# Score products over all 128 rows, a stacked gate product, and one engine for both block inversions in a one-core diffusion trunk step

## The chip, the cores and the metric

The kernel runs on one core of a Trainium2 chip, in one launch. The metric is the time of one execution on the device in microseconds (us), the median of several runs; lower is better.

## The reference, cut to what matters

One inference step of a two-layer trunk over 1152 tokens of width 1024: 128 context tokens and a 64 by 16 grid of 1024 latent tokens. Layer 0 mixes with neighbourhood attention (mixer A, 8 heads of 64) beside a bidirectional gated linear attention (mixer B); layer 1 with windowed grouped-query attention with a sink (mixer C) beside a bidirectional gated DeltaNet (mixer D). Each layer ends in a gated convolutional FFN. What the change touches is this:

```python
# mixers A and C, per block of 128 queries and per head
s = einsum(q, k) * scale (+ bias or mask)      # local keys and 128 cached keys
p = softmax(s);  o = einsum(p, v)

# mixer B: gates of both directions from a rank-16 projection
z = einsum('btzr,zrc->btzc', glr, w_g2) + b_g
g = log_sigmoid(z) / 16

# mixer D: per chunk of 64 tokens, a unit lower triangular solve
m_mat = tril(k_beta @ k.T * gam, -1) + eye(64)
sol = triangular_solve(m_mat, rhs)             # forward and time-flipped
```

Everything is computed to fp32 accuracy.

## The kernel before, in words

**Accuracy.** The large products keep fp32 accuracy by splitting: a value is rounded to fp32r (`hi`), the remainder goes into a second tile (`lo`), and a product is `hi*hi + hi*lo + lo*hi` in three TensorE passes of one array pass each (`gemm8`, lines 156 to 158). Plain fp32 operands make a matmul of two passes, which the trace shows as two records.

**Order of the program.** `even_a` (mixer A), `even_b` (mixer B), half of the output projection, FFN 0, `odd_1` (projections of C and D, preparation of D, block inversions), `odd_2` (mixer C, with the second half of the inversions between its units), `odd_3` (the recurrence of D), output projection, FFN 1. Instructions are written by Python generators; `weave` (line 322) interleaves a main generator with a filling one by the costs that they yield, and `mix` (line 1864) takes turns by fixed numbers. Where `manual_schedule` names an engine, that engine's instructions keep the written order; elsewhere the framework orders them by written priority and its own estimate. Inside a queue (TensorE = PE, VectorE = DVE, ScalarE = ACT, GpSimd = POOL, SyncE = SP, which issues most DMAs) everything runs in order.

**Attention (lines 524 to 643).** A head pair shares 128 partitions, head i on rows 64i to 64i+63. For each head, `stack_q` puts the rounded q on its own 64 rows of `qs[i]` and the remainder on the other 64; `stack_k` puts the rounded k on both halves of `ks[i]`, and the remainder of k on the head's 64 rows of one tile `kl` that the two heads share. `scores` then makes each piece of a score with two products: line 541 over 128 rows (`qs` against `ks`), and line 542 over the head's 64 rows only (`q[r:r+64]` against `kl[r:r+64]`). A unit is one block of 128 queries for two heads: score pieces for head 0, then head 1; DVE adds bias and takes the maximum (596), ACT exponentiates (606), DVE scales (621), PE transposes (630), ACT copies the transposes into a `pt` tile (632, four buffers), PE multiplies with v (641). Per head pair there are nine units: the context block with one piece of 128 keys, block 0 with pieces of 256 and 128, blocks 1 to 6 with 384 and 128, block 7 with one piece of 384. Four head pairs make 36 units in A and 36 in C. With depth 2, a unit's transposes come two units after its scores. In A, projections of the next pair fill between the units, and at the start of each pair the bias tiles are rebuilt from two tables: `rpb` by 8 DMAs (837) into a buffer of its own, the mask by one DMA per head (839), added on DVE (842).

**Gates of B (lines 887 to 970).** `narrow` makes the 32 rows of `glr`, ACT copies them (896) into a tile of 33 rows whose last row is 1 (892); `zgen` multiplies it in plain fp32 with `wz` (33 rows, 945), three pieces for each of two directions and four head pairs: 24 products. The weights of the projections go through the shared tiles `wraw`, `whi` and `wlo`, two buffers each.

**Block inversion of D (`inv`, lines 1362 to 1395).** For each head pair p the 32 by 32 diagonal blocks of 36 chunk matrices are inverted by elimination, 72 blocks on 72 partitions: 31 steps of one multiplication (1390) and one subtraction (1392), for the forward direction (d = 0) on DVE and for the backward one (d = 1) on POOL. `prep` writes the matrices out with POOL DMAs (1360, `am_dram`), `inv` reads the blocks back with SP DMAs (1375, `sysM`), and writes the inverses with POOL DMAs (1395, `n_dram`). The inversion of pair p-1 fills beside the preparation of pair p (`side`, 1413). The last one, `inv(3)`, runs in `odd_1`'s tail beside the last projections and the rotary products (`rope`, 1441 to 1445), with DVE and POOL in written order. The tile `X` of the next `prep` (1290) has the buffer of `am`, so it waits for the `am_dram` DMA. In `odd_2`, `merge` transposes the inverses (1512) and completes them with products (1518) between C's units.

Of the kernel before, what the change touches and what calls it, by code (L numbers as in the profile page):

```python
# [8 lines left out]
F32 = mybir.dt.float32  # L9
# [43 lines left out]
class Net:  # L53
    def __init__(self, ctx, tc, I, O, dbg=None):
# [38 lines left out]
        self.half = {}  # L93
        self.dvec = {n: self.const(f"dvec_{n}", [128, 18, 8]) for n in ("eG", "eE", "dl", "be")}

# [435 lines left out]
    def stack_k(self, ps, src, i, ks, kl, dst):  # L531
        nc = self.nc
        r, o = 64 * i, 64 * (1 - i)
        hi = dst(ks[r:r + 64])
        nc.scalar.copy(hi, src(ps[r:r + 64]))
        nc.scalar.copy(dst(ks[o:o + 64]), src(ps[r:r + 64]))
        nc.vector.tensor_tensor(out=dst(kl[r:r + 64]), in0=src(ps[r:r + 64]), in1=hi.bitcast(F32), op=ALU.subtract)

    def scores(self, s, off, q, ks, kl, r, c0, n, first, last):
        mm = self.nc.tensor.matmul  # L540
        mm(s[:, off:off + n], q, ks[:, c0:c0 + n], start=first, stop=False, skip_group_check=True)  # L541
        mm(s[:, off:off + n], q[r:r + 64], kl[r:r + 64, c0:c0 + n], start=False, stop=last, skip_group_check=True)  # L542

    def attn(self, mp, units, fill, depth=1):
# [5 lines left out]
        while q1 or q2 or not end:  # L550
# [14 lines left out]
            if u is not None:  # L565
                s = []
                for i in range(2):
                    t = self.pmt("s")
                    segs = u["segs"]
                    off = 0  # L570
                    for x, (c0, n) in enumerate(segs):
                        self.scores(t, off, u["q"][i], u["ks"][i], u["kl"], 64 * i, c0, n, x == 0, x == len(segs) - 1)
                        off += n
                    s.append(t)
                u["s"], u["nk"] = s, off
# [192 lines left out]
    def even_a(self, mp):  # L768
# [8 lines left out]
        def proj_a(p):  # L777
            qs = [mp.tile([128, T], F32R, name="qs", tag=f"qs{i}", bufs=2) for i in range(2)]
            ks = [mp.tile([128, 1280], F32R, name="ks", tag=f"ks{i}", bufs=2) for i in range(2)]
            kl = mp.tile([128, 1280], F32R, name="kl", tag="kl", bufs=2)  # L780
            kf = mp.tile([128, 128], F32, name="kf", tag="kf", bufs=1)
            ck = mp.tile([128, 128], F32, name="ck", tag="ck", bufs=1)
            nc.sync.dma_start(ck, I["akT"][p])
# [14 lines left out]
            def ev_k(b, ps):  # L798
                for o, n, t0 in IPIECES[b]:
                    if t0 < TP:  # L800
                        nc.scalar.copy(kf, ps[:, o:o + n])
                        nc.sync.dma_start(self.O["nak"][p], kf)
# [26 lines left out]
        def units():  # L829
            for p in range(4):  # L830
# [3 lines left out]
                bias = [mp.tile([128, 1280], F32, name="bias", tag=f"bias{i}", bufs=1) for i in range(2)]  # L834
                rb = mp.tile([128, 2, 384], F32, name="rpb", tag="rpb", bufs=1)
                for cl in range(8):
                    nc.sync.dma_start(rb[16 * cl:16 * cl + 16], I["rpbx"][2 * p:2 * p + 2, :, (7 - cl) * 16:(7 - cl) * 16 + 384].rearrange("h r k -> r h k"))
                for i in range(2):
                    nc.sync.dma_start(bias[i], I["maskA"])
                    for (b0, n0), (r0, n) in zip(VAR, ((0, 384), (128, 256), (0, 256))):  # L840
                        d = bias[i][:, b0:b0 + n]
                        nc.vector.scalar_tensor_tensor(out=d, in0=rb[:, i, r0:r0 + n], scalar=8.0, in1=d, op0=ALU.mult, op1=ALU.add)
                oT = mp.tile([128, T], F32, name="oT", tag="oT", bufs=1)
# [43 lines left out]
    def even_b(self, mp):  # L887
        nc, I = self.nc, self.I
        mm = nc.tensor.matmul
        self.wq = nc.scalar  # L890
        glr = mp.tile([33, T], F32, name="glr", tag="glr", bufs=1)
        nc.vector.memset(glr[32:33, :], 1.0)

        def glr_ev(b, ps):
            for o, nn, t0 in IPIECES[b]:
                nc.scalar.copy(glr[0:32, t0:t0 + nn], ps[:32, o:o + nn])

        wz = mp.tile([33, 2, 512], F32, name="wz", tag="wz", bufs=1)
        nc.sync.dma_start(wz, I["wz"])
        rst = mp.tile([128, T], F32, name="rst", tag="rst", bufs=1)  # L900
# [292 lines left out]
    def odd_1(self, mp, zp):  # L1193
# [168 lines left out]
        def inv(p):  # L1362
# [15 lines left out]
            for jj in range(31):  # L1378
                for d in range(2):
                    M, N, tmp = sy[d]  # L1380
                    eng = nc.vector if d == 0 else nc.gpsimd
                    if d == 0:
# [87 lines left out]
    def odd_2(self, mp, zp):  # L1470
# [17 lines left out]
        ks = [mp.tile([128, 1280], F32R, name="ks", tag=f"cks{i}", bufs=1) for i in range(2)]  # L1488
        kl = mp.tile([128, 1280], F32R, name="kl", tag="ckl", bufs=1)
        ck = mp.tile([128, 128], F32, name="ck", tag="cck", bufs=1)  # L1490
# [770 lines left out]
def build(tc, I, O):  # L2261
    with ExitStack() as ctx:
# [3 lines left out]
        def popen(name):  # L2266
            st = ExitStack()
            return st, st.enter_context(tc.tile_pool(name=name, bufs=1))
# [8 lines left out]
        for l in range(2):  # L2277
            if l:
                with tc.tile_pool(name="mz", bufs=2) as zp:
                    with tc.tile_pool(name="md", bufs=2) as mp:  # L2280
                        n.odd_1(mp, zp)
                    with tc.tile_pool(name="mc", bufs=2) as mp:
                        n.odd_2(mp, zp)
# [48 lines left out]
            ns.close()  # L2332
            xs.close()
        banks.close()

# [24 lines left out]
```

## Time and profile before

| what | us |
|---|---|
| median of 3 runs (3481.23 to 3495.96) | 3494.06 |
| the profiled execution | 3488.37 |
| its span in the profile | 3485.9 |
| PE busy / PE weight loads busy | 3321.6 / 3074.4 |
| DVE busy / ACT busy / POOL busy | 2035.4 / 1427.7 / 810.3 |
| mean granted TensorE clock of the profiled execution | 0.968 |

A granted clock of 1.00 is 2.4 GHz and 0.50 is 1.2 GHz; a value between is a mix over the stretch. An engine's share of the whole span says little here, because the stages have different limits; each is read by itself. In rows of the timeline the difference between the starts of two products is what a product costs in the queue; the length printed beside it overlaps the next one.

### The profile page before, as it was taken

Reading aid. Unit: us, or ns where it says so; the run is one execution under the profiler, and the core shown is the slowest. Engines: PE = TensorE matmul, PEld = TensorE weight load, DVE = VectorE, ACT = ScalarE, POOL = GpSimd, SP = SyncE. Lnnn points to the kernel's source line nnn. Section 1 sums busy time; section 2 is a strip of 40 time slices with the busy share of each in tenths; the row PEclk is TensorE's granted clock in tenths of the full one; section 3 lists DMA queues with packets and bytes.
Section 4 is the critical chain, followed back from the end, with each engine's and each line's share of the span. In section 5 each row is a group of like instructions: output and inputs, shape, how many; then the busy total and the mean of one; then the engine's idle time right before and its main releaser. Section 6 shows DMA issues by size and latency. Waiting matters only on the chain.

```text
span 3485.9 us, 58431 instructions
## 1 busy us (share of the span) xinstructions
PE 3321.6 (95%) x23095; PEld 3074.4 (88%) x23095; DVE 2035.4 (58%) x4040; ACT 1427.7 (41%) x3259; POOL 810.3 (23%) x1064
## 2 busy tenths in 40 slices
PE   6999999999999999999899977999989999999997
PEld 4988787889999999999798876777889999999997
DVE  5244577557555555555757776665676554444556
ACT  3345445545644444442554444551353222222223
POOL 1000001102644554450306585002310000000002
PEclk8999998999999999999999988999999999999999
DMA  5311233143322222221224444206410111111111
GB/s 178 100 55 43 72 116 105 58 159 111 93 82 83 85 77 80 83 89 47 85 73 116 113 121 126 52 15 219 153 46 29 44 43 37 42 44 43 43 43 67
DMA packets 186235, 285.18 MB, mean 82 GB/s; under 512 B 84043, under 2 KB 128203, under 8 KB 185836
## 3 DMA queue, kind: packets, MB, share of 16 engines
q1 hardware_dynamic: 152716, 228.03, 20.6%
q10 hardware_dynamic: 29264, 38.69, 3.6%
q0 software_dynamic: 3984, 14.75, 1.6%
q8 instruction: 183, 3.00, 0.4%
q14 instruction: 88, 0.72, 0.1%
HBM read 233.04 MB, written 48.37 MB: 81 GB/s over the span
## 4 chain that ended last, share of the span: by engine, by line
PE 79%; POOL 6%; DVE 5%; DMA 3%; issue 3%; ACT 2%; SPq 1%; DVEq 0%; POOLq 0%; ACTq 0%
PE g L156 14%; PE g L157 14%; PE g L158 14%; PE g L2060 5%; PE g L2058 5%; PE g L2059 5%; PE g L1895 4%; POOL sysN L1392 3%; POOL syst L1390 2%; PE s L542 2%; PE s L541 2%; PE ptr L630 2%; PE pvo L641 2%; PE kqs L1666 1%; PE g L1518 1%
## 5 line engine op out<-in xcount | busy, mean ns | idle before, releaser
L156 PE MATMUL g<-hh,whi 128*128 128x386 f32 (+2 forms) x3264 | 1126.8, 345 | 18.4 <-ACT df L1408 12.8
L158 PE MATMUL g<-hh,wlo 128*128 128x386 f32 (+2 forms) x3264 | 1112.5, 341 | 6.0 <-DVE wlo L144 6.0
L157 PE MATMUL g<-hl,whi 128*128 128x386 f32 (+2 forms) x3264 | 1116.4, 342 | 1.7 <-DVE hl L424 1.7
L156 PEld LDWEIGHTS g<-hh,whi 128*128 128x128 f32 x3264 | 623.3, 191 | 32.3 <-ACT df L1408 13.1
L158 PEld LDWEIGHTS g<-hh,wlo 128*128 128x128 f32 x3264 | 621.7, 190 | 8.2 <-DVE wlo L144 6.3
L157 PEld LDWEIGHTS g<-hl,whi 128*128 128x128 f32 x3264 | 622.1, 191 | 5.7 <-DVE hl L424 2.4
L1969 DVE SCALAR_TENSOR_TENSOR u<-g,cw,u 128x384 f32<-128x384 f32 (+1 forms) x264 | 163.2, 618 | 532.0 <-ACT u L1968 531.7
L1968 ACT ACTIVATE u<-g,cw 128x384 f32<-128x384 f32 (+1 forms) x264 | 153.7, 582 | 769.2 <-PE g L158 769.2
L516 DVE SCALAR_TENSOR_TENSOR x<-g,ada,x 128x128 f32<-128x128 f32 (+1 forms) x608 | 294.6, 512 | 204.5 <-PE g L2060 190.1
L141 ACT CAST whi<-wraw 128x1024 fp32r<-128x1024 f32 (+2 forms) x202 | 201.2, 996 | 443.9 <-PE g L2059 239.0
L2059 PE MATMUL g<-gl,whi 128*128 128x384 f32 (+1 forms) x1008 | 341.6, 339 | 1.9 <-DVE gl L2024 1.9
L2058 PE MATMUL g<-gh,whi 128*128 128x384 f32 (+1 forms) x1008 | 342.9, 340 | 0.2
L2060 PE MATMUL g<-gh,wlo 128*128 128x384 f32 (+1 forms) x1008 | 342.6, 340 | 0.0
L144 DVE TENSOR_TENSOR wlo<-wraw,whi 128x1024 fp32r<-128x1024 f32 (+2 forms) x214 | 255.0, 1192 | 103.6 <-ACT whi L141 103.5
L297 POOL TENSOR_TENSOR adat<-wada,adas 128x384 f32<-128x384 f32 x168 | 174.4, 1038 | 318.4 <-DMA wada<-in_adaw 288.5
L297 POOL TENSOR_TENSOR wada<-wada,adas 128x384 f32<-128x384 f32 x168 | 190.1, 1132 | 13.2
L2059 PEld LDWEIGHTS g<-gl,whi 128*128 128x128 f32 x1008 | 191.1, 190 | 2.4 <-issue 2.4
L2058 PEld LDWEIGHTS g<-gh,whi 128*128 128x128 f32 x1008 | 191.0, 189 | 0.8 <-issue 0.8
L2060 PEld LDWEIGHTS g<-gh,wlo 128*128 128x128 f32 x1008 | 190.1, 189 | 0.0
L2005 POOL MEMSET gh<- 128x1 f32 x44 | 4.3, 99 | 781.3 <-PE g L2060 776.7
L1970 DVE SCALAR_TENSOR_TENSOR u<-g,cw,u 128x384 f32<-128x384 f32 (+1 forms) x264 | 163.3, 619 | 9.3
L1895 PE MATMUL g<-hh,whi 128*128 128x384 f32 (+1 forms) x384 | 114.6, 364 | 5.0 <-DVE x L516 4.8
(369 smaller groups left out, 4988.6 us busy)
## 6 DMA issues: line engine op xcount, KB each, us to landing
wraw<-in_ffnup SPq DMA_DIRECT2D x88, 512.0 KB
wada<-in_adaw ACTq DMA_DIRECT2D x112, 192.0 KB
wada<-in_adaw SPq DMA_DIRECT2D x80, 256.0 KB
wraw<-in_wi SPq DMA_DIRECT2D x38, 512.0 KB
kq<-kq_dram SPq DMA_DIRECT2D x36, 512.0 KB
wraw<-in_ffndn SPq DMA_DIRECT2D x40, 384.0 KB
wada<-in_adaw ACTq DMA_DIRECT2D x56, 128.0 KB
wraw<-in_wi ACTq DMA_DIRECT2D x12, 512.0 KB
```

Of the source, the lines that this page charges most:

```text
L141: nc.scalar.copy(hi[:, :n], raw[:, :n])
L144: nc.vector.tensor_tensor(out=lo[:, c], in0=raw[:, c], in1=hi[:, c].bitcast(F32), op=ALU.subtract)
L156: mm(ps[:, :n], w, ah[:, k, c0:c0 + n], start=(k == 0), stop=False)
L157: mm(ps[:, :n], w, al[:, k, c0:c0 + n], start=False, stop=False)
L158: mm(ps[:, :n], lo[:, k * 128:(k + 1) * 128], ah[:, k, c0:c0 + n], start=False, stop=(k == 7))
L297: nc.gpsimd.tensor_tensor(out=d[:, :m], in0=w[:, :m], in1=sb[:, j, sl], op=ALU.mult)
L516: nc.vector.scalar_tensor_tensor(out=xr[:, t:t + nn], in0=ps[:, o:o + nn], scalar=gate[:, m, j:j + 1], in1=xr[:, t:t + nn], op0=ALU.mult, ...
L1895: mm(ps[:, :n], a[:, w], src[:, 2 * k + j, c0:c0 + n], start=(k + x == 0), stop=(k + x == 5))
L1970: nc.vector.scalar_tensor_tensor(out=t, in0=ps[:, 2:n], scalar=w[:, 2:3], in1=t, op0=ALU.mult, op1=ALU.add)
L2058: mm(ps[:, :n], hi[:, o:o + 128], gh[:, c0:c0 + n], start=(s == 0), stop=False)
L2059: mm(ps[:, :n], hi[:, o:o + 128], gl[:, c0:c0 + n], start=False, stop=False)
L2060: mm(ps[:, :n], lo[:, o:o + 128], gh[:, c0:c0 + n], start=False, stop=(s == ng - 1))
```

## The change

Five edits:

1. The remainder of k gets one tile per head (`kl[0]`, `kl[1]`), zero on the other head's 64 rows (memset on POOL), and line 542's product runs over all 128 rows against the whole `qs[i]`.
2. In A, to make room, the staging tiles `ck`, `kf` and `rpb` become buffers of the `pt` ring, and `rpb` is loaded per head (16 DMAs of one head each per pair, where there were 8 of two heads).
3. The gate product of B is one fp32r product over 98 rows: rounded `glr`, its remainder, rounded `glr` again and two rows of ones, against rounded weights, rounded weights, the weights' remainder, the rounded bias and its remainder. Building the weight tile takes 5 DMAs, one ACT copy, two DVE subtractions, one DVE copy and one DMA inside the core's memory, through a `wraw` and a `wlo` buffer; each piece of `glr` takes one more ACT copy and one DVE subtraction.
4. Both directions of the block inversion run on DVE.
5. The `dvec` tiles move from the constant pool into a pool that is open only in layer 1.

```diff
-        nc.vector.tensor_tensor(out=dst(kl[r:r + 64]), in0=src(ps[r:r + 64]), in1=hi.bitcast(F32), op=ALU.subtract)
+        nc.vector.tensor_tensor(out=dst(kl[i][r:r + 64]), in0=src(ps[r:r + 64]), in1=hi.bitcast(F32), op=ALU.subtract)
+    def new_kl(self, mp, tag, bufs):
+        kl = [mp.tile([128, 1280], F32R, name="kl", tag=f"{tag}{i}", bufs=bufs) for i in range(2)]
+        for i in range(2):
+            o = 64 * (1 - i)
+            self.nc.gpsimd.memset(kl[i][o:o + 64].bitcast(F32), 0.0)
+        return kl
-    def scores(self, s, off, q, ks, kl, r, c0, n, first, last):
+    def scores(self, s, off, q, ks, kl, c0, n, first, last):
         mm = self.nc.tensor.matmul
         mm(s[:, off:off + n], q, ks[:, c0:c0 + n], start=first, stop=False, skip_group_check=True)
-        mm(s[:, off:off + n], q[r:r + 64], kl[r:r + 64, c0:c0 + n], start=False, stop=last, skip_group_check=True)
+        mm(s[:, off:off + n], q, kl[:, c0:c0 + n], start=False, stop=last, skip_group_check=True)
...
-            kl = mp.tile([128, 1280], F32R, name="kl", tag="kl", bufs=2)
-            kf = mp.tile([128, 128], F32, name="kf", tag="kf", bufs=1)
-            ck = mp.tile([128, 128], F32, name="ck", tag="ck", bufs=1)
+            kl = self.new_kl(mp, "kl", 2)
+            ck = mp.tile([128, 512], F32, name="ck", tag="pt", bufs=4)[:, :128]
...
+                        kf = mp.tile([128, 512], F32, name="kf", tag="pt", bufs=4)[:, :128]
...
-                rb = mp.tile([128, 2, 384], F32, name="rpb", tag="rpb", bufs=1)
-                for cl in range(8):
-                    nc.sync.dma_start(rb[16 * cl:16 * cl + 16], I["rpbx"][2 * p:2 * p + 2, :, (7 - cl) * 16:(7 - cl) * 16 + 384].rearrange("h r k -> r h k"))
                 for i in range(2):
+                    rb = mp.tile([128, 512], F32, name="rpb", tag="pt", bufs=4)
+                    for cl in range(8):
+                        nc.sync.dma_start(rb[16 * cl:16 * cl + 16, :384], I["rpbx"][2 * p + i, :, (7 - cl) * 16:(7 - cl) * 16 + 384])
                     nc.sync.dma_start(bias[i], I["maskA"])
...
-        glr = mp.tile([33, T], F32, name="glr", tag="glr", bufs=1)
-        nc.vector.memset(glr[32:33, :], 1.0)
+        glr = mp.tile([98, T], F32R, name="glr", tag="glr", bufs=1)
+        nc.vector.memset(glr[96:98, :].bitcast(F32), 1.0)
...
-                nc.scalar.copy(glr[0:32, t0:t0 + nn], ps[:32, o:o + nn])
-        wz = mp.tile([33, 2, 512], F32, name="wz", tag="wz", bufs=1)
-        nc.sync.dma_start(wz, I["wz"])
+                c, src = slice(t0, t0 + nn), ps[:32, o:o + nn]
+                nc.scalar.copy(glr[0:32, c], src)
+                nc.scalar.copy(glr[64:96, c], src)
+                nc.vector.tensor_tensor(out=glr[32:64, c], in0=src, in1=glr[0:32, c].bitcast(F32), op=ALU.subtract)
+        raw = self.wpool.tile([128, 1024], F32, name="wraw", tag="wraw")
+        wzv = I["wz"].rearrange("p d n -> p (d n)")
+        for r in range(3):
+            nc.sync.dma_start(raw[32 * r:32 * r + 32], wzv[0:32])
+        for r in range(2):
+            nc.sync.dma_start(raw[96 + r:97 + r], wzv[32:33])
+        wz = mp.tile([98, 2, 512], F32R, name="wz", tag="wz", bufs=1)
+        wf = wz.rearrange("p d n -> p (d n)")
+        nc.scalar.copy(wf, raw[:98])
+        low = self.wpool.tile([128, 1024], F32R, name="wlo", tag="wlo")
+        nc.vector.tensor_tensor(out=low[64:96], in0=raw[64:96], in1=wf[64:96].bitcast(F32), op=ALU.subtract)
+        nc.vector.tensor_tensor(out=low[96:98], in0=raw[96:98], in1=wf[96:98].bitcast(F32), op=ALU.subtract)
+        nc.vector.tensor_copy(wf[64:96], low[64:96].bitcast(F32))
+        nc.sync.dma_start(wf[97:98].bitcast(F32), low[97:98].bitcast(F32))
...
-                    eng = nc.vector if d == 0 else nc.gpsimd
+                    eng = nc.vector
...
-        kl = mp.tile([128, 1280], F32R, name="kl", tag="ckl", bufs=1)
+        kl = self.new_kl(mp, "ckl", 1)
```

## Rows read from the trace of the kernel before

**Rows 1.** Page, part 4: the chain that ended last, by engine.
```profile
PE 79%; POOL 6%; DVE 5%; DMA 3%; issue 3%; ACT 2%; SPq 1%; DVEq 0%; POOLq 0%; ACTq 0%
```
**Rows 2.** Windows by stage: length, busy us (count) of PE, PEld, DVE, ACT, POOL; clock; DMA.
```profile
140.00:376.50 236.50, 236.50 (x1467) 203.05 (x1466) 116.75 (x329) 118.21 (x296) 0.00 (x0) 1.00 0.17 53
376.50:418.00 41.50, 41.50 (x316) 29.39 (x315) 26.97 (x89) 24.33 (x62) 0.00 (x0) 1.00 0.07 28
440.00:712.00 272.00, 260.75 (x1722) 221.62 (x1723) 194.81 (x407) 148.43 (x272) 31.14 (x30) 0.92 0.31 98
1840.00:1922.00 82.00, 76.81 (x559) 70.63 (x558) 64.13 (x123) 34.78 (x51) 51.36 (x73) 0.96 0.42 111
...
2069.00:2128.60 59.60, 47.37 (x249) 47.05 (x250) 55.50 (x71) 23.18 (x51) 54.72 (x68) 0.86 0.23 79
...
2165.00:2362.00 197.00, 187.89 (x2111) 141.56 (x2108) 120.78 (x371) 106.61 (x311) 13.88 (x70) 0.93 0.12 33
```
**Rows 3.** Timeline of PE in mixer A: head 0's scores, head 1's first product, transposes.
```profile
387.75 0.45 PE L541 MATMUL s<-ks,qs 128*128 128x384 f32 x1
388.12 0.44 PE L542 MATMUL s<-kl,qs 64*128 64x384 f32 x1
388.49 0.33 PE L541 MATMUL s<-ks,qs 128*128 128x128 f32 x1
388.75 0.32 PE L542 MATMUL s<-kl,qs 64*128 64x128 f32 x1
389.00 0.44 PE L541 MATMUL s<-ks,qs 128*128 128x384 f32 x1
...
393.94 1.09 PE L630 MATMUL ptr<-ident,sc 128*128 128x128 f32 x8
```
**Rows 4.** Timeline of PE in mixer A: two neighbouring products of a projection.
```profile
238.51 0.34 PE L158 MATMUL g<-hh,wlo 128*128 128x384 f32 x1
238.69 0.34 PE L156 MATMUL g<-hh,whi 128*128 128x384 f32 x1
```
**Rows 5.** Groups of instructions, line 542 in mixer A (150 to 420 us).
```profile
L542 PE MATMUL s<-kl,qs 64*128 64x128 f32 (+2 forms) x128 | 48.3, 377 | 0.0
```
**Rows 6.** The same view in mixer C (2140 to 2372 us).
```profile
L542 PE MATMUL s<-kl,qs 64*128 64x128 f32 (+2 forms) x128 | 51.6, 403 | 0.0
```
**Rows 7.** Waits of PE in mixer C: total us, times, longest.
```profile
PE g L1518 <- DVE dT L1512: 9.1, 3, 3.6
```
**Rows 8.** Timeline of POOL around mixer A's end.
```profile
421.04 1.06 POOL L901 MEMSET rst<- 128x1152 f32 x1 [342.11 <-DMA o_dram<-oT]
```
**Rows 9.** Tile rpb: its DMA issues on SP, min/median/max ns.
```profile
L837 SPq DMA_DIRECT2D rpb<-in_rpbx x32: 328/422/1968, 123.7 to 308.7; - x32
```
**Rows 10.** Timeline of PE in mixer B: two gate products (four records), then a projection.
```profile
433.92 1.55 PE L945 MATMUL z<-glr,wz 33*128 33x384 f32 x4
435.40 0.44 PE L156 MATMUL g<-hh,whi 128*128 128x384 f32 x1
```
**Rows 11.** Windows 1840 to 2130 us of line 1390 alone: the sum.
```profile
sum 290.00, DVE 65.36 POOL 85.18; mean DVE 9.34 POOL 12.17
```
**Rows 12.** The same for line 1392.
```profile
sum 290.00, DVE 70.84 POOL 89.94; mean DVE 10.12 POOL 12.85
```
**Rows 13.** Timeline of DVE, the first inversion: smallest step, one size early and late.
```profile
1841.41 0.20 DVE L1390 TENSOR_TENSOR syst<-sysM,sysN 72x31 f32<-72x31 f32 x1
...
1848.23 0.37 DVE L1392 TENSOR_TENSOR sysN<-sysN,syst 72x207 f32<-72x207 f32 x1
...
1879.47 0.68 DVE L1392 TENSOR_TENSOR sysN<-sysN,syst 72x207 f32<-72x207 f32 x1
```
**Rows 14.** Timeline of POOL behind the first inversion.
```profile
1895.29 0.58 POOL L1395 DMA_DIRECT2D n_dram<-sysN  x1 [0.30 <-POOL sysN L1392]
...
1904.06 0.58 POOL L1360 DMA_DIRECT2D am_dram<-am  x1
```
**Rows 15.** Waits of DVE from 1840 to 2130 us.
```profile
DVE X L1290 <- DMA am_dram<-am: 23.1, 4, 8.7
```

More of the change, by code (lines that the diff above doesn't have):

```diff
@@ L93, in __init__ @@
         self.half = {}
-        self.dvec = {n: self.const(f"dvec_{n}", [128, 18, 8]) for n in ("eG", "eE", "dl", "be")}
     def banks(self, g, m):
@@ L571, in attn @@
                     for x, (c0, n) in enumerate(segs):
-                        self.scores(t, off, u["q"][i], u["ks"][i], u["kl"], 64 * i, c0, n, x == 0, x == len(segs) - 1)
+                        self.scores(t, off, u["q"][i], u["ks"][i], u["kl"][i], c0, n, x == 0, x == len(segs) - 1)
                         off += n
@@ L841, in units @@
                         d = bias[i][:, b0:b0 + n]
-                        nc.vector.scalar_tensor_tensor(out=d, in0=rb[:, i, r0:r0 + n], scalar=8.0, in1=d, op0=ALU.mult, op1=ALU.add)
+                        nc.vector.scalar_tensor_tensor(out=d, in0=rb[:, r0:r0 + n], scalar=8.0, in1=d, op0=ALU.mult, op1=ALU.add)
                 oT = mp.tile([128, T], F32, name="oT", tag="oT", bufs=1)
@@ L890, in even_b @@
         self.wq = nc.scalar
-        glr = mp.tile([33, T], F32, name="glr", tag="glr", bufs=1)
-        nc.vector.memset(glr[32:33, :], 1.0)
+        glr = mp.tile([98, T], F32R, name="glr", tag="glr", bufs=1)
+        nc.vector.memset(glr[96:98, :].bitcast(F32), 1.0)
         def glr_ev(b, ps):
             for o, nn, t0 in IPIECES[b]:
-                nc.scalar.copy(glr[0:32, t0:t0 + nn], ps[:32, o:o + nn])
-        wz = mp.tile([33, 2, 512], F32, name="wz", tag="wz", bufs=1)
-        nc.sync.dma_start(wz, I["wz"])
+                c, src = slice(t0, t0 + nn), ps[:32, o:o + nn]
[16 more added lines that the diff above has]
+        nc.sync.dma_start(wf[97:98].bitcast(F32), low[97:98].bitcast(F32))
+        low = raw = None
         rst = mp.tile([128, T], F32, name="rst", tag="rst", bufs=1)
@@ L2278, in build @@
             if l:
+                ds, dp = popen("dvec")
+                n.dvec = {k: dp.tile([128, 18, 8], F32, name=f"dvec_{k}", tag=k) for k in ("eG", "eE", "dl", "be")}
                 with tc.tile_pool(name="mz", bufs=2) as zp:
@@ L2333, in build @@
             xs.close()
+            if l:
+                ds.close()
         banks.close()
```

## The prediction

> **What bounds the kernel now.** I read the chain of waits first, for the engines on the path that sets the end [rows 1]: PE has 79%, and POOL, busy for under a quarter of the span, has 6%. POOL can be on a path only where something runs there alone, so next come the windows by stage [rows 2]. In mixer A (140 to 418 us) PE is busy 236.5 of 236.5 and 41.5 of 41.5 us at a granted clock of 1.00, with DVE and ACT at about half and POOL at 0: PE is the bound there, and any time that its queue loses is worth its full length. In mixer B (440 to 712) PE has 260.8 of 272 and DVE 194.8. In mixer C (2165 to 2362) PE has 187.9 of 197, DVE 120.8, ACT 106.6. The inversions (1840 to 2129) differ: DVE and POOL are both loaded, 64.1 and 51.4 of 82 us in the first period, 55.5 and 54.7 of 59.6 in the last, and PE is idle 5.2 and 12.2 us of these.
>
> The timeline of PE in a unit of A gives the key [rows 3]. The four starts 387.75, 388.12, 388.49, 388.75 and the next head's 389.00 make steps of 0.37, 0.37, 0.26 and 0.25 us: 384 keys cost 0.37, 128 keys 0.255. In a projection, two neighbours of 384 columns over all 128 rows start 0.18 us apart [rows 4]. A score product of the same length costs twice that, in line 541 (128 rows) as much as in line 542 (64 rows): what costs is not the rows used but the alternation between the two shapes.
>
> **Edit 1, scores.** Afterwards all score products have the projections' shape. For 384 keys I take the 0.18 of rows 4. For 128 keys no full-height fp32r product stands in a row; the nearest is the transpose, 128 columns over 128 rows, eight in 1.09 us [rows 3], so 0.136. The ends: 0.18, if a short piece is no cheaper than a long one, and 0.06, if cost goes with columns alone (128/384 of 0.18). I take 0.136, which was measured at this length. For 256 keys, halfway: 0.31 before, 0.158 after.
>
> - Blocks 1 to 6: before 4 x 0.37 + 4 x 0.255 = 2.50 us, after 4 x 0.18 + 4 x 0.136 = 1.26; 1.24 saved.
> - Block 0: 2.27 to 1.18, 1.09 saved. Context: 1.02 to 0.54, 0.48. Block 7: 1.48 to 0.72, 0.76.
> - A head pair: 6 x 1.24 + 1.09 + 0.48 + 0.76 = 9.8 us; four pairs 39 us for A's 128 products of line 542 and as many of line 541 [rows 5]. Ends: 33 (0.18 throughout) and 49 (0.06).
>
> In A PE is the bound, so it counts in full, less what edit 2 costs. Cover left: A shrinks from 278 to 239 us with 144 us of DVE and 143 of ACT; in the part without projections 41.5 falls to about 32 with 27 on DVE. So PE stays the bound.
>
> In C line 542 has the same 128 products at 403 ns busy each against A's 377 [rows 6, 5], 7% dearer because of half-clock stretches: 39 x 1.07 = 42 us. Against that stand PE's waits for the transposes of the merges, 9.1 us in 3 [rows 7]. Two or so units lie between the last product of one merge and the first of the next; with each 1.24 us shorter, the wait grows by about 2.5 us, three times 7.5. C gets 34. Ends: 20, if every wait doubles and is followed by as much at the half clock, and 50. DVE then has 121 of 163 us, and is late next.
>
> The new memsets (half a tile of 1280 columns, 8 in A, 2 in C) cost POOL about 1.1 us each, as one of 1152 columns did [rows 8]. POOL had idled 342 us there: nothing in A. In C's opening two of them precede the keys, 0 to 2 us; taken as 0, since the queue waits for loads then.
>
> **Edit 2, staging in the pt ring.** Per pair SP issues 16 `rpb` DMAs instead of 8, at 0.42 us each [rows 9]: 3.4 us more, and they now wait for the product that frees a `pt` buffer. Queued behind them are the second mask load, the bias additions on DVE, and the next maxima. At the first three pairs projections lie between the units and hide it; at the last there is nothing, so 3.4 us (ends 0 and 10, if the ACT copies into `pt` stall at every pair). The `ck` and `kf` uses hold a buffer for one load or store and cost nothing while projections follow. A: 39 - 3 = 36 us gained.
>
> **Edit 3, gates.** Two products as four records start at 433.92 and release the next at 435.40 [rows 10]: 0.74 us each, against 0.18 for one full-height fp32r product of 384 columns. 24 x 0.56 = 13 us on a PE that is 96% busy. Building the weight tile lies beside `narrow` and the first projection, 13 us from the memory's release at 421.04 [rows 8] to the first gate product at 433.92; its casts and subtractions are some 4 us and its DMAs some 4. But it holds a `wraw` and a `wlo` buffer through which the next weights come: 0 to 6 us, taken as 3. The four extra copies and subtractions of `glr` lie there too. B: 10 us; ends 2 and 15.
>
> **Edit 4, inversion.** POOL loses 85.2 + 89.9 = 175 us, DVE has 65.4 + 70.8 = 136 us for its half [rows 11, 12]. DVE's steps last 0.20 us for 31 elements and 0.37 for 207, but 0.68 for the same 207 once POOL is at its large steps [rows 13]. Alone, a step is thus 0.17 us + 0.97 ns per element. The sizes j(32 - j) sum to 5456 over 31 steps: 10.6 us per line, 21.1 per direction, 169 for all eight. DVE gets 169 - 136 = 33 us more, where it idled 17.9 us in the first period and 4.1 in the last [rows 2]. What goes: at the first inversion's end POOL issues the inverse at 1895.29, and the `am_dram` write only at 1904.06, 8.8 us later behind memsets that wait for DMAs [rows 14]; DVE's next preparation waits 23.1 us for such writes [rows 15]. With no chain on POOL that write can go when its data is ready. Ends: 33 us lost, if none of the extra work fits into DVE's idle time; about 35 gained, if PE's idle time goes (5.2 and 12.2 in the two shown periods, four periods at their mean). Nearest to the rows is the chain itself: a period has 31 us of other DVE work (64.1 less a quarter of 136) and 42 of inversion, 73 of 82. I take 5 us gained. Waiting afterwards: the projections' evictions on DVE, behind the steps, and PE behind those.
>
> Edit 5 moves memory and costs nothing.
>
> **Sum.** 36 + 34 + 10 + 5 = 85 us off the profiled execution's 3488.4 (span 3485.9 and 2.5 around it): 3403. The median of the runs shown is 5.7 us above that execution, so 3409 for a median.
>
> **A page against it.** In the trace a 64-row product costs as much as a 128-row one of the same length [rows 3]. "TensorEngine Tiling (Array Packing)" in the Trainium skill, section "Tiling Modes" with its table of speedups, has a contraction of 64 rows run as two independent tiles, up to twice as fast. By that rule widening would give up a gain; here each 64-row product stands between two full-height ones, and the steps show none. The same page's "Mode switching requires drain" is what the trace agrees with.
>
> **The rivals.**
> 1. *DVE or latency takes over in A and C.* For: DVE would be at 27 of 32 us in A's last part and 74% in C. Against: depth 2 leaves a whole unit between. Half the scores' gain: 3409 + 35 = 3444. Chance 0.12.
> 2. *DVE becomes the bound of the inversions.* For: 55.5 of 59.6 us already. Against: much of that is the doubled steps. The loss of 33 instead of a gain of 5: 3447. Chance 0.12.
> 3. *The scores keep their cost*, the doubled step being due to something other than the shapes, say the short accumulation groups: 3409 + 36 + 34 = 3479, unchanged within what can be told. Against: the projections' products swap their stationary tile as often, at 0.18 [rows 4]. Chance 0.05.
> 4. *Slower: the inversion's steps run ahead of everything in DVE's queue.* All 169 us then lie on the path uncovered, PE's evictions waiting: 3409 + 169 = 3578. It decides from the point where more than 85 + 17 of the 169 us, 60%, lie uncovered. Against: the framework orders by written priority and the steps are written in small groups. Chance 0.03.
> 5. *The 64-row products are half price today*: widening adds 128 + 128 products at about 0.15 us, 39 us, and the scores gain nothing: 3479 + 39 = 3518. The steps of rows 3 speak against it. Chance 0.01.
> 6. *The inversions give back all of PE's idle time*: 3409 - 30 = 3379. Chance 0.07.
>
> **How the numbers follow.** The forecast has 0.60; its own range, from the ends of the scores' price, edit 2, edit 3 and C's waits, is 3383 to 3435. Taking in rivals 1, 2 and 6 makes 3370 to 3450. A measurement of this kernel can tell about 0.5%, 17 us, from no change. Faster by more: the forecast and rivals 1, 2 and 6, 0.91; the same: rival 3, 0.05; slower: rivals 4 and 5, 0.04.
>
> **What would show it.** Right: score products 0.18 apart for 384 keys and about 0.14 for 128, all as 128 rows; A shorter by about 36 us with PE still at 100%; C by about 34; 24 gate records instead of 48; inversion steps on DVE at 0.37 us for 207 elements, POOL nearly empty, and 1840 to 2129 no longer than now. Wrong: steps of 0.25 us and more between score products, PE idle in A, or a stretch from the first inversion to C longer by over 15 us.

## The result, and the profile after

The changed kernel takes 3394.89 us (median of 4 runs, 3387.07 to 3396.72), the kernel before 3494.32 (median of 4): a ratio of 0.972, 95% interval 0.969 to 0.975. The profiled execution takes 3394.25 us with a span of 3392.5, so 93.4 us of span are gone. The forecast was 85 us, 3409, in a range of 3370 to 3450. By the medians 99.4 us are gone, so the sum is 9% short by the spans and 14% by the medians, and two of its four terms (B and the inversions) are far off.

To see where the time went, I follow the same landmarks through both traces: the starts of the first and the last instruction on a tile. First the kernel before, then after (tile view: line, engine, operation, count; shortest, median and longest ns; first and last start in us; forms).

```profile
L542 PE MATMUL s<-kl,qs x256: 322/382/687, 156.8 to 2353.3; 64*128 64x384 f32 x104, 64*128 64x256 f32 x16, 64*128 64x128 f32 x8
L856 SPq DMA_DIRECT2D o_dram<-oT x4: 326/352/378, 246.5 to 418.0; - x4
L945 PE MATMUL z<-glr,wz x48: 481/587/1006, 433.9 to 683.2; 33*128 33x384 f32 x48
L1390 DVE TENSOR_TENSOR syst<-sysM,sysN x124: 186/542/911, 1841.4 to 2120.6; 72x31 f32<-72x31 f32 x8, 72x60 f32<-72x60 f32 x8, 72x87 f32<-72x87 f32 x8, 72x112 f32<-72x112 f32 x8
L1392 POOL TENSOR_TENSOR sysN<-sysN,syst x124: 246/628/3277, 1847.2 to 2126.5; 72x31 f32<-72x31 f32 x8, 72x60 f32<-72x60 f32 x8, 72x87 f32<-72x87 f32 x8, 72x112 f32<-72x112 f32 x8
L1512 DVE STREAM_TRANSPOSE dT<-tv x8: 1334/1351/1370, 2156.8 to 2303.5; 128x1152 f32<-128x1152 f32 x8
```

```profile
L549 PE MATMUL s<-kl,qs x256: 272/307/525, 153.1 to 2263.5; 128*128 128x384 f32 x104, 128*128 128x256 f32 x16, 128*128 128x128 f32 x8
L863 SPq DMA_DIRECT2D o_dram<-oT x4: 326/336/349, 229.6 to 380.3; - x4
L968 PE MATMUL z<-glr,wz x24: 335/442/687, 406.5 to 648.1; 98*128 98x384 f32 x24
L1413 DVE TENSOR_TENSOR syst<-sysM,sysN x248: 174/353/423, 1806.3 to 2075.1; 72x207 f32<-72x207 f32 x10, 72x247 f32<-72x247 f32 x10, 72x175 f32<-72x175 f32 x9, 72x231 f32<-72x231 f32 x9
L1415 DVE TENSOR_TENSOR sysN<-sysN,syst x248: 173/354/2555, 1806.6 to 2075.3; 72x207 f32<-72x207 f32 x10, 72x252 f32<-72x252 f32 x10, 72x87 f32<-72x87 f32 x9, 72x175 f32<-72x175 f32 x9
L1535 DVE STREAM_TRANSPOSE dT<-tv x8: 1334/1350/1369, 2107.7 to 2226.0; 128x1152 f32<-128x1152 f32 x8
```

| stretch, by these rows | before | after | saved | forecast |
|---|---|---|---|---|
| start to first score | 156.8 | 153.1 | 3.7 | 0 |
| mixer A: first score to the last write of its output | 261.2 | 227.2 | 34.0 | 39 - 3 |
| B's opening: that write to the first gate product | 15.9 | 26.2 | -10.3 | -3 |
| first to last gate product | 249.3 | 241.6 | 7.7 | 13 |
| to the first inversion step (with FFN 0) | 1158.2 | 1158.2 | 0.0 | 0 |
| first to last inversion step | 285.1 | 269.0 | 16.1 | 5 |
| to C's first merge transpose | 30.3 | 32.4 | -2.1 | 0 |
| C: first merge transpose to last score | 196.5 | 155.8 | 40.7 | 34 |
| rest | 1132.6 | 1129.0 | 3.6 | 0 |

The first and the last line can't be told from chance: in the kernels below the first score lies between 153 and 160 us, and the rest takes 1128 to 1133 us, also where nothing there was changed. The others are taken up one by one.

**The scores' price.** PE's timeline of an inner unit of A, beside [rows 3]:

```profile
359.79 0.44 PE L548 MATMUL s<-ks,qs 128*128 128x384 f32 x1
360.07 0.33 PE L549 MATMUL s<-kl,qs 128*128 128x384 f32 x1
360.24 0.22 PE L548 MATMUL s<-ks,qs 128*128 128x128 f32 x1
360.30 0.27 PE L549 MATMUL s<-kl,qs 128*128 128x128 f32 x1
360.41 0.39 PE L548 MATMUL s<-ks,qs 128*128 128x384 f32 x1
360.64 0.33 PE L549 MATMUL s<-kl,qs 128*128 128x384 f32 x1
360.98 1.06 PE L637 MATMUL ptr<-ident,sc 128*128 128x128 f32 x8
```

From 359.79 to the transposes at 360.98 are 1.19 us, before 2.50 and by the forecast 1.26. A 384-key product behind another one steps by 0.17, a 128-key one by 0.06 (360.24 to 360.30), the lower end of what I had allowed; the first product behind a head's short pieces or behind `pvo` loses 0.06 to 0.1 more (0.28 and 0.23). The errors nearly cancel.

**The stages by window** (columns as in [rows 2]): A with projections, A's last pair, B, the inversions, C.

```profile
140.00:345.00 205.00, 204.88 (x1481) 195.81 (x1480) 115.48 (x331) 119.39 (x297) 4.63 (x4) 1.00 0.17 52
345.00:380.00 35.00, 30.57 (x279) 25.68 (x278) 23.37 (x84) 21.43 (x57) 0.00 (x0) 0.90 0.11 39
400.00:672.00 272.00, 255.69 (x1741) 228.10 (x1739) 195.84 (x415) 145.43 (x272) 29.90 (x30) 0.92 0.31 96
1805.00:2077.00 272.00, 241.51 (x1712) 222.39 (x1711) 238.35 (x644) 125.39 (x211) 43.20 (x39) 0.93 0.42 114
2105.00:2265.00 160.00, 143.02 (x2067) 127.94 (x2067) 120.83 (x374) 104.41 (x305) 13.55 (x68) 0.91 0.20 50
```

PE is full in A up to 345 us and no longer in the last pair: 30.6 of 35 us, clock 0.90, where [rows 2] have 41.5 of 41.5 at 1.00. POOL has 43 us in all the inversions, where it had over 50 in each period.

**Two new waits of PE.** At A's last pair SP issues this (an xN row is N instructions; the number before its name is their length):

```profile
335.33 0.33 SPq L846 DMA_DIRECT2D bias<-in_maskA  x1
337.04 8.35 SPq L845 DMA_DIRECT2D rpb<-in_rpbx  x16
345.50 0.37 SPq L846 DMA_DIRECT2D bias<-in_maskA  x1
```

The second mask load stands behind sixteen `rpb` loads, 8.35 us. DVE's additions to the bias wait for it, the maxima stand behind them, and PE's next transposes wait with these:

```profile
349.42 1.23 DVE L849 SCALAR_TENSOR_TENSOR bias<-rpb,bias 128x384 f32<-128x384 f32 x3 [1.76 <-DMA bias<-in_maskA]
```

PE's waits, there and again in B's opening:

```profile
353.49 0.69 PE L637 MATMUL ptr<-ident,sc 128*128 128x128 f32 x2 [4.25 <-DVE sc L628]
...
388.16 0.53 PE L890 MATMUL g<-hh,wlo 128*32 128x386 f32 x1 [8.35 <-DVE wlo L143]
388.49 0.53 PE L888 MATMUL g<-hh,whi 128*32 128x386 f32 x1
```

4.25 us at the last pair, 8.35 before `narrow`'s third kind of product, whose weights are L143's `wlo`; and then the products step by 0.33 (388.16, 388.49) in place of 0.175, at half clock. The engines that make `wlo` show why:

```profile
383.15 1.04 ACT L916 CAST wz<-wraw 98x1024 fp32r<-98x1024 f32 x1 [4.39 <-DMA o_dram<-oT]
```

```profile
383.44 1.02 DVE L899 MEMSET glr<- 2x1152 f32 x1 [3.21 <-DMA o_dram<-oT]
384.49 1.22 DVE L918 TENSOR_TENSOR wlo<-wraw,wz 32x1024 fp32r<-32x1024 f32 x1
385.73 1.22 DVE L919 TENSOR_TENSOR wlo<-wraw,wz 2x1024 fp32r<-2x1024 f32 x1
386.99 0.69 DVE L920 CAST wz<-wlo 32x1024 fp32r<-32x1024 f32 x1
387.68 0.42 DVE L143 TENSOR_TENSOR wlo<-wraw,whi 128x256 fp32r<-128x256 f32 x1
```

The gate's tiles `wz` and `glr` lie in memory that A's output `oT` frees only when its last DMA has landed (4.39 us of waiting for ACT's cast, 3.21 for DVE's memset). The memset, two subtractions behind ACT's cast, and a copy stand in DVE's queue ahead of `narrow`'s own subtraction, which takes 0.42 us and needs none of that memory.

### The profile page after: what moved, and what is told of

Same layout as the page of the kernel before. It is cut to its first block, busy times and chain, and to the rows that moved or that the text cites. A ratio compares the mean times of both kernels' runs of the same rounds, so it can differ in the third digit from the quotient of the medians.

```text
span 3392.5 us, 58498 instructions
## 1 busy us (share of the span) xinstructions
PE 3215.9 (95%) x23071; PEld 3049.1 (90%) x23071; DVE 2053.3 (61%) x4295; ACT 1431.2 (42%) x3264; POOL 657.2 (19%) x826
## 4 chain that ended last, share of the span: by engine, by line
PE 80%; DVE 9%; ACT 4%; DMA 3%; issue 2%; POOL 1%; SPq 1%; DVEq 0%; POOLq 0%; ACTq 0%
PE g L155 16%; PE g L156 15%; PE g L157 15%; PE g L2083 5%; PE g L2081 5%; PE g L2082 5%; PE g L1918 4%; PE pvo L648 1%; PE ptr L637 1%; PE kqs L1689 1%; DVE sysN L1415 1%; DMA wada<-in_adaw 1%; PE s L548 1%; PE g L1541 1%; PE s L549 1%
## 5 line engine op out<-in xcount | busy, mean ns | idle before, releaser
L143 DVE TENSOR_TENSOR wlo<-wraw,whi 128x1024 fp32r<-128x1024 f32 (+2 forms) x214 | 257.2, 1203 | 97.5 <-ACT whi L140 97.3
```

Of the source, the lines that this page charges most:

```text
L143: nc.vector.tensor_tensor(out=lo[:, c], in0=raw[:, c], in1=hi[:, c].bitcast(F32), op=ALU.subtract)
```

## The experiments

Each kernel is the changed one with the edit shown, measured beside the kernel before. The changed kernel's 3394.9 is the measure; times are medians.

**1. The shape of the second score product**: its 64 rows again (the tile per head stays), cut here to the line that counts, and then, also over 64 rows, with the pieces in another order.

```diff
-        mm(s[:, off:off + n], q, kl[:, c0:c0 + n], start=False, stop=last, skip_group_check=True)
+        mm(s[:, off:off + n], q[r:r + 64], kl[r:r + 64, c0:c0 + n], start=False, stop=last, skip_group_check=True)
```

> The changed kernel with the second score product over the head's 64 rows again (one tile per head kept). Theory (each change between a 64-row and a 128-row product costs about 0.18 us): the steps between score products go back to about 0.37 us for 384 keys and 0.255 for 128; mixer A gets about 36 us longer, mixer C about 40, and the time is about 3395 + 76 = 3471. Rival (64-row products are cheaper in themselves): below 3395. Rival (short groups of products cost, not shapes): no difference, 3395.

```diff
                     for x, (c0, n) in enumerate(segs):
-                        self.scores(t, off, u["q"][i], u["ks"][i], u["kl"][i], c0, n, x == 0, x == len(segs) - 1)
+                        nc.tensor.matmul(t[:, off:off + n], u["q"][i], u["ks"][i][:, c0:c0 + n], start=(x == 0), stop=False, skip_group_check=True)
+                        off += n
+                    off, r = 0, slice(64 * i, 64 * i + 64)
+                    for x, (c0, n) in enumerate(segs):
+                        nc.tensor.matmul(t[:, off:off + n], u["q"][i][r], u["kl"][i][r, c0:c0 + n], start=False, stop=(x == len(segs) - 1), skip_group_check=True)
                         off += n
```

> As half_rows, but per head all 128-row products come first and then all 64-row ones: in an inner unit 4 changes of shape where there were 8. Theory (the change costs, not the 64-row product): half of the loss stays, in an inner unit 4 x 0.18 = 0.7 us, and the time is about 3395 + 38 = 3433; a 64-row product right behind another one steps at about 0.1 to 0.18 us. Rival (every 64-row product is dear in itself): the same as half_rows, about 3471.

half_rows takes 3487.3 us (3477.0 to 3496.9; ratio to before 0.998, 0.996 to 0.9995), half_rows_grouped 3437.5 (ratio 0.984, 0.980 to 0.988). Grouped, two products of 384 and 128 keys are one row of the timeline of PE in A:

```profile
364.54 0.51 PE L579 MATMUL s<-ks,qs 128*128 128x384 f32 x2
364.98 0.50 PE L583 MATMUL s<-kl,qs 64*128 64x384 f32 x2
365.41 0.51 PE L579 MATMUL s<-ks,qs 128*128 128x384 f32 x2
365.84 0.50 PE L583 MATMUL s<-kl,qs 64*128 64x384 f32 x2
```

A pair of 384 and 128 keys steps by 0.43 to 0.44 us, the 64-row pair as long as the 128-row pair. At 0.18 and 0.06 the two products alone are 0.24; the rest, 0.19, is one change of shape, if both directions cost the same. The same price comes out of [rows 3]: 0.37 less 0.18, and 0.255 less 0.06. So a 64-row product costs what a 128-row one does, and a change between them 0.19 us at either length. This settles rivals 3 and 5 of the prediction. "TensorEngine Tiling (Array Packing)" in the Trainium skill, section "Key Properties", says that a change of the tiling mode drains the engine. These runs agree in that a change costs, 0.19 us each; a drain as such no row shows.

Taking the rows back cost 92 us, though, where 76 were expected and A and C had gained 75. In half_rows' trace A lasts 273.3 us (158.2 to 431.5), 12 more than before the change. The windows at A's last pair show why:

```profile
390.00:400.00 10.00, 10.00 (x36) 6.20 (x36) 3.90 (x14) 4.61 (x15) 0.00 (x0) 0.52 0.15 60
400.00:410.00 10.00, 10.00 (x35) 6.59 (x35) 3.89 (x13) 2.58 (x6) 0.00 (x0) 0.50 0.01 2
410.00:420.00 10.00, 10.00 (x62) 7.07 (x60) 4.64 (x16) 5.07 (x12) 0.00 (x0) 0.78 0.00 0
```

The clock is at 0.5 for some 24 us, from 389.9, where a wait of 1.2 us ends (`ptr` for `sc`, behind the bias), to 414, while PE is busy throughout. In the changed kernel the half clock after the longer wait lasted from 353.5 to about 359. If the wait is the cause, this part belongs to edit 2, which the next runs test.

**2. The queue at A's last pair.** Half of the `rpb` loads go to POOL, which is idle there.

```diff
-                        nc.sync.dma_start(rb[16 * cl:16 * cl + 16, :384], I["rpbx"][2 * p + i, :, (7 - cl) * 16:(7 - cl) * 16 + 384])
+                        (nc.sync, nc.gpsimd)[i].dma_start(rb[16 * cl:16 * cl + 16, :384], I["rpbx"][2 * p + i, :, (7 - cl) * 16:(7 - cl) * 16 + 384])
```

> The changed kernel with head 1's eight rpb loads issued by POOL, which is idle there, so that the second mask load stands behind 8 DMAs on SP and not 16. Theory (PE's 4.25 us wait at A's last pair is that queue): the second mask load is issued 3.5 us earlier, the wait and the half clock behind it go, 5 to 7 us, and the time is 3388 to 3390. Rival (the loads wait for pt buffers, whichever queue issues them): 3394 to 3396.

> half_rows with the edit of rpb_pool. Open: taking edit 1 back cost 92 us, where mixers A and C had gained 75 from it. Theory (the short wait for the bias at A's last pair drops the clock, and products of alternating shapes take 25 us at half clock to win it back): without that wait the clock stays at 1.00 there, A lasts 258 to 264 us as in the kernel before, in place of 273, and the time is 3473 to 3479. Rival (the longer A is the alternation itself): A stays at 270 us and more, 3483 to 3488.

rpb_pool takes 3392.6 us (3388.4 to 3399.9): by the time alone not told from the changed kernel. By the stage, A lasts 223.3 us (158.6 to 381.9) in place of 227.2, and PE's wait for `sc` there is down from 4.2 to 0.7: 4 us in all, less than the 5 to 7 expected (PE now waits 1.8 us for `ri`). half_rows_rpb takes 3480.4 (3467.8 to 3493.2), just above its expected range, and its A lasts 262.1 us (158.9 to 421.0) in place of 273.3, at a clock of 1.00 throughout. So the 11 us in A were the wait and the clock after it. They are not the whole surplus: the medians differ by only 7 us, with spreads of 20 and 25, and C too is longer than its 196.5 us before the change, 206.4 in half_rows' profiled execution (clock 0.86; the slowest of its ten) and 199.5 in half_rows_rpb's (0.90, before 0.91). Why C's clock differs is open.

Between these two kernels, neither with that wait, A differs by 38.8 us; the forecast for its scores was 39. C differs by 43.7 (199.5 against 155.8, from the tile rows of `dT` and `s`).

**3. The gates.** First edit 3 taken back whole; then kept, with `narrow`'s weights loaded and split ahead of it.

```diff
-        glr = mp.tile([98, T], F32R, name="glr", tag="glr", bufs=1)
+        glr = mp.tile([33, T], F32, name="glr", tag="glr", bufs=1)
...
-        wz = mp.tile([98, 2, 512], F32R, name="wz", tag="wz", bufs=1)
+        wz = mp.tile([33, 2, 512], F32, name="wz", tag="wz", bufs=1)
+        nc.sync.dma_start(wz, I["wz"])
```

> The changed kernel with the plain fp32 gate product of 33 rows again. Theory (what the 24 cheaper products save is lost in the opening of mixer B, where the weights of narrow's products wait behind the building of the gate's weight tile): from the last write of A's output to the first gate product 16 us in place of 26, and 7 to 8 us more from the first to the last gate product; the time is 3390 to 3396, no slower. The prediction's price for this edit: 10 us, 3405.

```diff
-    def narrow(self, src, dst):
+    def narrow(self, src, dst, w=None):
...
-        hi, lo = self.wchunk(src, 256)
+        hi, lo = w or self.wchunk(src, 256)
...
         self.wq = nc.scalar
+        wn = self.wchunk(I["wglr"], 256)
         glr = mp.tile([98, T], F32R, name="glr", tag="glr", bufs=1)
...
-        for _ in self.narrow(I["wglr"], glr_ev):
+        for _ in self.narrow(None, glr_ev, wn):
```

> The changed kernel with the weights of narrow's products loaded and split ahead of the building of the gate's weight tile. Theory (PE's 8.35 us wait for L143's wlo and the half clock after it come from that order alone): from the last write of A's output to the first gate product 10 to 16 us in place of 26, and the time is 3379 to 3386. Rival (the building itself takes that long, the weight tile being in memory that A frees): the wait moves to the first gate product, 3392 to 3395.

old_gate takes 3384.1 us (ratio 0.968, 0.965 to 0.971), gate_late 3377.9 (0.967, 0.965 to 0.969). Their gate products and last writes:

```profile
L863 SPq DMA_DIRECT2D o_dram<-oT x4: 327/327/345, 234.0 to 382.9; - x4
L952 PE MATMUL z<-glr,wz x48: 481/587/1005, 392.8 to 643.2; 33*128 33x384 f32 x48
```

```profile
L863 SPq DMA_DIRECT2D o_dram<-oT x4: 327/327/344, 231.1 to 380.0; - x4
L969 PE MATMUL z<-glr,wz x24: 335/441/687, 394.8 to 635.9; 98*128 98x384 f32 x24
```

| | changed | old_gate | gate_late |
|---|---|---|---|
| A's last write to first gate product | 26.2 | 9.9 | 14.8 |
| first to last gate product | 241.6 | 250.4 | 241.1 |

Edit 3 as written lost 11 us: its products save 8.8 us and its opening costs 16.3, 7.5 in all. (11 is by the medians; the two profiled executions, old_gate's the slowest of its four, differ by 6.) By the order alone 17 us come back. More than the wait of 8.35 goes, because with its weights ready `narrow` has issued 37 of its 72 products by 356 us, where the changed kernel had 6 before A's last write: they fill PE's wait at the last pair, which is gone in gate_late (0.6 us, for something else). So the late weights cost twice, and they made edit 2's wait visible. With the order repaired, edit 3 is worth 6 us by the medians (3384.1 to 3377.9); their runs overlap, so this is no more than an estimate.

**4. The inversion.** The backward half on POOL again; then the same with the writes of the chunk matrices on SP.

```diff
-                    eng = nc.vector
+                    eng = nc.vector if d == 0 else nc.gpsimd
```

> The changed kernel with the backward inversion on POOL again. Theory (the gain is the am_dram writes that had stood behind POOL's chain, and DVE's steps that were doubled beside POOL): the stretch from the first to the last inversion step, 269 us now, gets 16 us longer, DVE waits some 20 us for am_dram again, and the time is about 3411. The prediction's price for this edit: 5 us, 3400. Rival (one engine for both is no gain, the gain of that stretch came from elsewhere): 3395 or less.

```diff
             for o, t in out:
-                nc.gpsimd.dma_start(o, t)
+                nc.sync.dma_start(o, t)
```

> As inv_pool (backward inversion on POOL), but the writes of am, aq and tt to DRAM are issued by SP in place of POOL, so that they don't stand behind POOL's chain. Theory A (the wait of X for those writes was the cost): DVE's waits for am_dram go, the two middle periods lose 9 us together, and the time is about 3402. Theory B (DVE's steps doubled beside POOL are the cost): about 3411 as inv_pool. If both count, about 3405, still above the 3395 of the changed kernel.

inv_pool takes 3410.6 us (ratio 0.976, 0.972 to 0.980), inv_pool_sp 3398.5 (0.973, 0.970 to 0.975). Tile X and DVE's waits for these writes (total us, times, longest), in inv_pool, in inv_pool_sp and in the changed kernel:

```profile
L1313 DVE TENSOR_TENSOR X<-dg,th x8: 1350/1358/1360, 1721.2 to 1960.7; 128x1152 f32<-128x1152 f32 x8
```

```profile
DVE X L1313 <- DMA am_dram<-am: 25.0, 5, 8.8
```

```profile
L1313 DVE TENSOR_TENSOR X<-dg,th x8: 1346/1348/1359, 1720.1 to 1944.2; 128x1152 f32<-128x1152 f32 x8
```

```profile
DVE X L1313 <- DMA am_dram<-am: 0.4, 1, 0.4
```

```profile
L1313 DVE TENSOR_TENSOR X<-dg,th x8: 1340/1350/1359, 1718.6 to 1945.0; 128x1152 f32<-128x1152 f32 x8
```

```profile
DVE X L1313 <- DMA am_dram<-am: 2.3, 1, 2.3
```

The edit is worth 15.7 us; 12 of them come as well by changing the queue of the writes and leaving the chain on POOL. The first to the last `X` are 239.5 us in inv_pool, 224.1 in inv_pool_sp, 226.4 in the changed kernel. So in these periods theory A holds and theory B doesn't: DVE's steps are slowed beside POOL in inv_pool_sp too (median of L1415 498 ns, 354 in the changed kernel), and the periods are no longer for it. From the last `X` to the last inversion step it is 132.7 us in inv_pool (to 2093.4), 138.1 in inv_pool_sp (to 2082.3), 130.3 in the changed kernel (to 2075.3): in the last inversion one engine is no worse than two. Why inv_pool_sp is longer there is open.

**5. Mixer C.** The products of a merge come one step of the weaving after its transposes; the yielded costs keep their sum.

```diff
             nc.vector.transpose(dT.rearrange("p c t -> p (c t)"), t.rearrange("p c t -> p (c t)"))
-            yield 0.0
+            yield 1.8 * d
...
-                yield 1.2
+                yield 1.05
```

> The changed kernel with the products of a merge one step of the weaving later than its two transposes (the cost that the generator yields is moved, its sum kept). Theory (mixer C's PE waits 17.1 us for dT because the products are queued straight behind the transposes): that wait falls below 6 us, the clock in C rises, and the time is 3380 to 3387. Rival (DVE is late with everything in C): PE waits as long, for sc, hh or pt, and the time is 3392 to 3398.

merge_early takes 3381.8 us (ratio 0.968, 0.966 to 0.970). PE's waits for `dT` in the changed kernel, and those in merge_early with its window of the middle of C:

```profile
PE g L1541 <- DVE dT L1535: 17.1, 4, 4.9
```

```profile
PE g L1541 <- DVE dT L1535: 1.3, 4, 0.7
```

```profile
2130.00:2250.00 120.00, 113.83 (x1751) 100.22 (x1751) 97.31 (x311) 86.30 (x254) 11.88 (x56) 1.00 0.16 43
```

The waits fall from 17.1 to 1.3 us, the clock in this window is 1.00, in the changed kernel 0.91, and C lasts 141.7 us (2106.3 to 2248.0) in place of 155.8.

**6. All three together** (the edits of gate_late, rpb_pool and merge_early), and two variants of that, the first with the edit of inv_pool_sp's writes.

> The changed kernel with the edits of gate_late, rpb_pool and merge_early together. Theory (three separate waits in three stages, so their gains add): 3395 less 17, 13 and 2 to 4, so 3361 to 3364. Rival (the stages hide each other's gains): above 3370.

> As combined, with the writes of am, aq and tt issued by SP. With both directions on DVE, nothing large stands on POOL any more, and DVE waits only 2.3 us for am_dram. Theory (moving the inversion has already taken these writes' delay away): within 4 us of combined. Rival (the two cures add, as both removed a different wait): 10 us and more below combined.

```diff
-            for _ in self.mix(t, iv, 1, 4):
+            for _ in self.mix(t, iv, 1, 3):
```

> As combined, with three steps of the last inversion in place of four behind each block of the last projections. Theory (DVE sets the pace of that stretch, 57 us busy of 67, so the order only moves the wait): within 4 us of combined, PE idle less among the blocks and more behind them. Rival (PE's idle time there comes from the evictions and weight splits behind the steps): 5 to 10 us below combined.

combined takes 3368.0 us (3364.5 to 3372.3; ratio 0.964, 0.962 to 0.967): faster than both kernels, 27 us below the changed one. That is 4 to 7 us less than expected, which fits what experiment 3 showed: gate_late already fills the wait that rpb_pool removes. combined_sp takes 3374.5 (0.966, 0.964 to 0.968): the two cures don't add, and it is 6 us above combined, outside the 4 expected. In its trace the first to the last `X` are 230.2 us, 226.3 in combined, with a wait of PE for an `X` of 4.7 us that combined doesn't have; what delays that `X` is open. combined_tail takes 3371.1 (0.965, 0.963 to 0.967), within 4 us as expected.

## Why the prediction was right, and where not

- **Edit 1, right, and for its reason.** The alternation costs, not the rows: 0.19 us for each change. In A 39 us were forecast and 38.8 measured between kernels without the other wait. That it agrees so closely is luck in part, as two wrong prices pull opposite ways: a short product costs 0.06 to 0.11, not 0.136, and the first one behind another shape 0.28, not 0.18; the unit came out at 1.19 against 1.26.
- **C, right in kind, 7 too low.** The two terms were 42 for the products and 7.5 for PE's waits on the merges' transposes. The term that was mis-sized is the second: the three waits of [rows 7] grew from 9.1 only to 12.3 us, by 3.2 (the fourth of the 17.1 is the first merge's, where PE idled 3.0 us before as well). With these some 40.7 + 3.2 = 44 us are the products', an estimate that leaves the clock aside. Rival 1, half of the scores' gain, did not come.
- **Edit 2, mechanism right.** 3 us forecast, 4 measured by the stage, by the very queue named. Not seen: the half clock after the wait, which with alternating shapes made it 11, and that "at the last there is nothing" holds only while `narrow`'s weights are late; in gate_late its products fill the wait.
- **Edit 3, wrong in sign.** 10 gained by the forecast, 11 lost when measured against old_gate. The failed step is "Building the weight tile lies beside `narrow` and the first projection": I counted how long the build takes and which buffers it holds, but not that it stands *ahead* of `narrow`'s own weight split in DVE's queue, nor that it waits until A's last DMA has landed. PE then stood 8.35 us for `wlo`, and 17 us came back with the order alone. The products' price was right: between the first and the last of them PE is busy 225.8 us, 238.7 before, 12.9 less where 13 were forecast. But the stretch is only 7.7 us shorter (8.8 against old_gate), because PE's idle time in it grew from 11.3 to 16.3 us, its waits for `ktok`, DVE's copy of the transposed keys, from 6.2 to 9.5. "A PE that is 96% busy" did not make the saving count in full.
- **Edit 4, mechanism right, size wrong.** 5 forecast, 15.7 measured. The wait for the `am_dram` writes was named, and it was what went. The step that failed set 33 us of added work on DVE against it (its "31 us of other DVE work" is 30 by its own numbers, which changes nothing). DVE's two lines do take 78.3 + 85.2 = 163.6 us (169 forecast, 136 before), but that lies beside PE's work: PE has 241.5 of 272 us in the window of the inversions. PE still waits there for ACT and DVE, so rival 6 came only half true; rival 2 fell.
- **Edit 5** was not tried alone; no row shows a cost.
- **The sum** came as near as it did by luck: errors cancel. By the table, B is 13 us short of its forecast, while C and the inversions (with the stretch behind them) exceed theirs by 7 and 9. The range is wide enough that it would have held with either error alone.

Open: why the stretch to C's first transpose is 2.1 us longer, why C's clock differs between the kernels with 64 rows, and what costs combined_sp its 6 us.

## What to carry to other kernels

When an operation is replaced by a cheaper one that needs preparation, look up what the preparation stands ahead of in each queue and whose memory it takes, not only how long it is. A wait of an engine for a DMA's completion may be a question of which queue issues it; change the queue before moving the computation. And count changes of a matmul's row shape, not rows: the same products in another order are already cheaper.

## What the runs showed of the hardware that was not expected

- A change between 64-row and 128-row products that alternate costs 0.19 us at 128 as at 384 columns; between full-height products a 128-column one steps by only 0.06 us. The first change behind a long run of full-height products was cheaper: in the kernel before, the context's first score product steps by 0.15 us (376.57 to 376.72), so 0.09 for the change.
- After a wait of only 1.2 us, a busy PE stayed at half clock for some 24 us while its products alternated in shape (half_rows). In half_rows_grouped, with half of the changes, it was 17 us (371 to 388) after a wait of 3.0; in the changed kernel, with none, it was back in some 6 us after a wait of 4.25. The order is that of the changes, but the waits differ too, and what decides it stays open.
